# Sliding-window attention beside its projections: both heads' value products in one step, wider splits, keys staged earlier, new step rates

## The chip, the cores and the metric

The kernel runs on one core of one Trainium2 chip. The metric is the device time of one execution in microseconds, median of several runs. The engines are TensorE (PE, with its weight loads shown as PEld), VectorE (DVE), ScalarE (ACT), GpSimd (POOL) and SyncE (SP), which issues the transfers.

## The reference, cut to what matters

The whole program is a two-layer block, a second mixing block and a final norm, all in float32. The change lies in the second layer of the first block ("layer b"), which is attention over a window of 128 tokens, 16 meta tokens and a sink, with a gate:

```python
q, gate = jnp.split(rms_norm(x, norm_g) @ w_in, 2, axis=-1)      # 512+16 tokens, 2048 + 2048 columns
q = partial_rope(q.reshape(B, L, B_Q_HEADS, B_HEAD_DIM), cos, sin)   # 32 query heads of 64, 4 key heads
sr = jnp.einsum('bnqkgd,bnskd->bnkgqs', qr, kb) * scale          # per chunk of 64 queries: 16 + up to 192 keys
sr = jnp.where(valid, sr, -jnp.inf)
pr = sink_softmax(sr, sink)       # exp(sc - m) / (sum exp(sc - m) + exp(sink - m))
orr = jnp.einsum('bnkgqs,bnskd->bnqkgd', pr, vb)
return x + (o * jax.nn.silu(gate)) @ w_out
```

## The kernel before, in words

**Products.** A float32 operand is split into a high part of a narrower format (made on ACT by a copy) and the remainder (made on DVE by a subtraction), and each product is made of three TensorE products: high by high, low by high, high by low. `split` is the helper (L470 on ACT, L471 on DVE; with a scale L473 and L474); the weights get the same at L377 and L378 in `w_split`.

**Units of layer b.** The projection runs in eight units, `q0 g0 q1 q2 g1 q3 g2 g3`: four q units (query columns of four head pairs each) and four g units (their gates). A unit has 4 tiles of 128 columns, a tile has 16 contraction steps of three 512-column products (`pj`); each contraction step ends with `K.tick()`, so a unit has 64 ticks. A tile's sum stands in one of three PSUM banks (`psj`, tag pj). A q tile is rotated on DVE into `f` (two buffers, L972 to L975) and then split into `qp` (L1154), of which there is one set for each of the two tile pairs and heads, shared by consecutive q units; so a q unit's splits wait until the attention of the unit before has made its last scores.

**Attention as a background.** `attention(u, qp)` is a generator. `K.tick` adds `K.rate` to a credit and runs one step of the generator in front for each whole credit. Its steps are, for each of 8 windows n: two transposing steps `trans(n, g)` (one for each of the two key heads g), the scores of window n + 2, and two value steps `values(n, 0)` and `values(n, 1)`. Scores go to one PSUM tile S, transposes to one of two tiles T, values of both heads to the two halves of one bank O (`psO`, one buffer). `values` makes four O products for windows of 208 keys (high and low weights, two key blocks), then copies half the result on ACT (L1116) and adds the other half on DVE into `K.H` (L1117). `K.pe.strict` ties the first projection product that follows a background step in program order behind that step's last TensorE instruction. Apart from such ties and from data, the framework orders the instructions of each engine ahead of the run, by program order and by what is ready in its own estimate; so a later background step may stand ahead of an earlier one that is blocked.

**Windows.** `windows(p)` runs in the background too, once for units 0 and 1 and once for units 2 and 3. It loads the pair's keys (`ke`, from DRAM scratch `kvd`), splits them with a scale (`kxh`, `kxl`), loads the values (`vx`), waits four steps, and transposes and splits the values into `vw`, two windows a step. `ke`, `vx` and the softmax weights `p` share a ring of two buffers (tag "p"). At a q unit's start all but the last background generator are run to their end at once (`while len(K.bg) > 1: K.step()`).

**Gates.** Once attention of unit u is done, each of its four H tiles is multiplied by its gate (L1167), 14 of the 16 on POOL.

Of the kernel before, what the change touches and what calls it, by code (L numbers as in the profile page):

```python
# [10 lines left out]
F32 = mybir.dt.float32  # L11
# [933 lines left out]
def layer_b(K, dbg):  # L945
    nc, tc, a = K.nc, K.tc, K.a
    with ExitStack() as c:
# [46 lines left out]
        for k in range(KT):  # L994
            K.split(K.OPH[:, k], K.OPL[:, k], K.H[:, k], scale=K.vcol("b_norm", k))

        kv = {}
        K.rate = 1 / 5
        done = set()
        pending = {}  # L1000
# [1 line left out]
        def windows(p):  # L1002

            ks = []
            for g in range(2):
                ke = bp.tile([P, TX], F32, tag="p", name="ke", bufs=2)
                for i in range(2):
                    nc.sync.dma_start(ke[64 * i:64 * i + 64], K.kvd[p][64 * g:64 * g + 64])
                kxh = bp.tile([P, TX], R, tag=f"kxh{g}", name="kxh")
                kxl = bp.tile([P, TX], R, tag=f"kxl{g}", name="kxl")  # L1010
                K.split(kxh, kxl, ke, scale=SC_B)
                ks.append((kxh, kxl))
            vx = bp.tile([P, TX], F32, tag="p", name="vx", bufs=2)
            nc.sync.dma_start(vx, K.kvd[2 + p])
            for _ in range(4):
                yield
            vw = bp.tile([P, 2, 8, 2, 2, 64], R, tag="vw", name="vw")
            kv[p] = (ks, vw)

            def vsplit(d, src):  # L1020
                v = src.rearrange("p (g c) -> p g c", g=2)
                K.split(d[:, :, 0], d[:, :, 1], v)
            for n in range(8):
                off, ln = WIN[n]
                t = psT.tile([P, 512], F32, tag="T", name="T")
                n0 = min(ln, P)
                K.pe.transpose(t[0:n0, 0:P], vx[:, off:off + n0], K.ident)
                if ln > P:
                    K.pe.transpose(t[0:ln - P, P:2 * P], vx[:, off + P:off + ln], K.ident)
                vsplit(vw[0:n0, 0, n], t[0:n0, 0:P])  # L1030
                if ln - P == 16:

                    nc.gpsimd.memset(vw[0:32, 1, n].bitcast(F32), 0.0)
                    src = t[0:16, P:2 * P].rearrange("p (g c) -> p g c", g=2)
                    hi, lo = vw[0:16, 1, n, :, 0], vw[0:16, 1, n, :, 1]
                    nc.scalar.activation(vw[32:48, 1, n, :, 0], src, AF.Copy)
                    K.split(hi, lo, src)
                    nc.vector.tensor_tensor(vw[32:48, 1, n, :, 1], src, hi.bitcast(F32), ALU.subtract)
                elif ln > P:
                    vsplit(vw[0:ln - P, 1, n], t[0:ln - P, P:2 * P])  # L1040
                if n % 2:
                    yield

        def attention(u, qp):
# [5 lines left out]
            def scores(n):  # L1050
                off, ln = WIN[n]
                ps = psS.tile([P, 2, 512], F32, tag="S", name="S")
                for g in range(2):
                    for t in range(2):
                        o, q = ps[:, g, t * ln:(t + 1) * ln], qp[t][g][:, P * n:P * n + P]
                        K.pe.matmul(o, q, ks[g][0][:, off:off + ln], start=True, stop=False)
                        K.pe.matmul(o, q, ks[g][1][:, off:off + ln], start=False, stop=True)
                v = ps[:, :, 0:2 * ln].rearrange("p g (t l) -> p g t l", t=2)
                nb = bp.tile([P, 4], F32, tag="nb", name="nb", bufs=2)
                sums = bp.tile([P, 4], F32, tag="sums", name="sums", bufs=2)  # L1060
                es = bp.tile([P, 4], F32, tag="es", name="es", bufs=2)
                pt = bp.tile([P, 4, 208], F32, tag="p", name="p", bufs=2)
                nc.vector.tensor_reduce(nb.rearrange("p (g t) -> p g t", g=2), v, AX.X, ALU.max, negate=True)
                nc.vector.tensor_tensor(nb, nb, ns, ALU.min)  # L1064
                nc.vector.tensor_tensor(es, nb, ns, ALU.subtract)
                for g in range(2):
                    for t in range(2):
                        j = 2 * g + t
                        K.act(pt[:, j, 0:ln], ps[:, g, t * ln:(t + 1) * ln], AF.Exp, bias=nb[:, j:j + 1],
                              accum_out=sums[:, j:j + 1])  # L1070
                K.act(es, es, AF.Exp)
                nc.vector.tensor_tensor(sums, sums, es, ALU.add)
                nc.vector.reciprocal(sums, sums)
                for j in range(4):
                    if j % 2:
                        nc.scalar.activation(pt[:, j, 0:ln], pt[:, j, 0:ln], AF.Copy, scale=sums[:, j:j + 1])
                    else:
                        nc.vector.tensor_scalar(pt[:, j, 0:ln], pt[:, j, 0:ln], sums[:, j:j + 1], None, ALU.mult)
                st[n] = pt

            def trans(n, g):
                off, ln = WIN[n]
                pt = st[n]
                t_ = psT.tile([P, 512], F32, tag="T", name="T")
                n0 = min(ln, P)
                ph = bp.tile([P, 2, 256], R, tag="ph", name="ph", bufs=2)
                pl = bp.tile([P, 2, 256], R, tag="pl", name="pl", bufs=2)
                for t in range(2):
                    K.pe.transpose(t_[0:n0, P * t:P * (t + 1)], pt[:, 2 * g + t, 0:n0], K.ident)
                    if ln > P:  # L1090
                        K.pe.transpose(t_[0:ln - P, 256 + P * t:256 + P * (t + 1)], pt[:, 2 * g + t, P:ln], K.ident)
                K.split(ph[0:n0, 0], pl[0:n0, 0], t_[0:n0, 0:256])
                if ln - P == 16:
                    nc.gpsimd.memset(ph[0:32, 1].bitcast(F32), 0.0)
                    K.split(ph[0:16, 1], ph[32:48, 1], t_[0:16, 256:512])
                elif ln > P:
                    K.split(ph[0:ln - P, 1], pl[0:ln - P, 1], t_[0:ln - P, 256:512])
                st[n, g] = (ph, pl)

            def values(n, g, po):  # L1100
                off, ln = WIN[n]
                ph, pl = st.pop((n, g))
                n0 = min(ln, P)
                o = po[:, 256 * g:256 * g + 256]
                for b in range(2 if ln > P else 1):
                    m = min(ln - P * b, P)
                    if m == 16:
                        K.pe.matmul(o, vw[0:48, b, n, g].rearrange("p h c -> p (h c)"), ph[0:48, b], start=False, stop=True)
                        continue
                    v = vw[0:m, b, n, g].rearrange("p h c -> p (h c)")  # L1110
                    K.pe.matmul(o, v, ph[0:m, b], start=(b == 0), stop=False)
                    K.pe.matmul(o, v, pl[0:m, b], start=False, stop=(b == (ln > P)))

                r = slice(64 * g, 64 * g + 64)
                vo = K.sumsq[:, 256 * (n % 2):256 * (n % 2) + 256].rearrange("p (j q) -> p j q", j=4)
                nc.scalar.activation(vo[r], o[64 - 64 * g:P - 64 * g].rearrange("p (j q) -> p j q", j=4), AF.Copy)  # L1116
                nc.vector.tensor_tensor(K.H[r, 4 * u:4 * u + 4, NM + 64 * n:NM + 64 * n + 64], vo[r],  # L1117
                                        o[r].rearrange("p (j q) -> p j q", j=4), ALU.add)
# [1 line left out]
            po = {}  # L1120
            seq = [[("s", 0)], [("s", 1)]] + [[]] * 3
            for n in range(8):
                seq += [[("t", n, 0)], [("t", n, 1)], [("s", n + 2)] if n < 6 else [], [("v", n, 0)], [("v", n, 1)]]
            for step in seq:
                for f, *x in step:
                    if f == "s":
                        scores(x[0])
                    elif f == "t":
# [6 lines left out]
            done.add(u)  # L1135
            for f in pending.pop(u, []):
                f()

        for un in UNITS_B:
            u = int(un[1])  # L1140
            if un[0] == "q":
                while len(K.bg) > 1:
                    K.step()
                if u % 2 == 0:
                    K.at(K.tickno + 12 + 1, lambda p=u // 2: K.bg.append(windows(p)))

                qp = [[bp.tile([P, 1024], R, tag=f"qp{g}", name="qp", bufs=2) for g in range(2)] for _ in range(2)]
                for j in range(4):
# [4 lines left out]
                        r, r2 = slice(64 * g, 64 * g + 64), slice(64 - 64 * g, P - 64 * g)  # L1153
                        K.split(x[r], x[r2], f[r, NM:T].rearrange("p (n q) -> p n q", n=8), eng=nc.vector)  # L1154
                K.at(K.tickno + 12, lambda u=u, qp=qp: K.bg.append(attention(u, qp)))
                K.rate = .46 if u < 3 else .52
                K.pe.strict = True
            else:
                for j in range(4):
# [3 lines left out]
                    K.act(th, f[:, NM:T], AF.Tanh, scale=0.5)  # L1163
                    nc.vector.scalar_tensor_tensor(th, th, 1.0, f[:, NM:T], ALU.add, ALU.mult)

                    def gate(th=th, dst=K.H[:, 4 * u + j, NM:T], e=nc.vector if u == 3 and j % 2 else nc.gpsimd):
                        e.tensor_tensor(dst, dst, th, ALU.mult)  # L1167
                    if u in done:
                        gate()
                    else:  # L1170
# [824 lines left out]
```

## Time and profile before

| What | Value |
|---|---|
| median of 3 runs | 2838.5 us (2836.59 to 2840.35) |
| the profiled execution: its own time | 2833.57 us |
| its span, first to last instruction | 2831.8 us |
| mean granted TensorE clock | 0.997 of full |
| busy: PE, DVE, ACT, POOL | 99%, 61%, 47%, 12% of the span |
| DMA | 278.64 MB, mean 98 GB/s |

Durations below come from the one profiled execution, which was 4.9 us shorter than the median of the runs. Times are counted from the start of its span. Layer b's eight units lie between about 1144 and 1605 us. A row of the timeline gives start, duration, engine, line, operation, tiles as out<-in, shapes, and in brackets how long the engine had sat idle before it and which instruction released it.

### The profile page before, as it was taken

The page shows a single profiled execution, that of the slowest core. Times are in us where ns is not written, and L with a number is a line of the kernel's source. Part 1 is how long each engine was busy: PE and PEld are TensorE (multiplying, and loading weights), DVE is VectorE, ACT ScalarE, POOL GpSimd, SP SyncE. Part 2 cuts the span into 40 slices and gives each one's busy share as a digit, 9 for nine tenths or more (in the row PEclk, how much of TensorE's full clock was granted, in tenths as well). Part 3 has the DMA queues.
Part 4 walks back from the last instruction along what each step waited for, and adds up shares of the span by engine and source line. Part 5 has one row for each costly group of instructions (what it writes and reads, how often), then busy time and mean ns, then how long its engine had stood idle before and what let it go on. Part 6 is the DMA issues. An engine that isn't in the chain of part 4 may idle for free. (4 is left out here: it accounts for less than half of the span.)

```text
span 2831.8 us, 45345 instructions
## 1 busy us (share of the span) xinstructions
PE 2790.1 (99%) x17576; PEld 2508.1 (89%) x17576; DVE 1713.6 (61%) x3551; ACT 1321.7 (47%) x2973; POOL 329.3 (12%) x362
## 2 busy tenths in 40 slices
PE   9999999999999999999999999999999999999997
PEld 9999999999999999888788888888888887878887
DVE  6555555556575555776767633565656489773375
ACT  5333334334354343564666533465555366552263
POOL 0000000000000110000000022132322134121103
PEclk9999999999999999999999999999999999999999
DMA  5222222222224445312222343322222223233331
GB/s 169 93 75 86 85 75 85 86 76 85 78 78 140 151 133 172 110 67 83 80 75 68 110 144 127 99 83 81 85 77 91 87 92 114 84 106 122 105 112 68
DMA packets 93897, 278.64 MB, mean 98 GB/s; under 512 B 10528, under 2 KB 18864, under 8 KB 93680
## 3 DMA queue, kind: packets, MB, share of 16 engines
q1 hardware_dynamic: 92720, 274.86, 29.9%
q8 instruction: 138, 2.26, 0.3%
q10 hardware_dynamic: 960, 0.87, 0.1%
q14 instruction: 79, 0.65, 0.1%
HBM read 257.11 MB, written 17.01 MB: 97 GB/s over the span
## 5 line engine op out<-in xcount | busy, mean ns | idle before, releaser
L258 PE MATMUL pj<-OPH,wh 128*128 128x264 f32 (+1 forms) x4416 | 1454.5, 331 | 10.1 <-ACT wh L377 6.6
L258 PE MATMUL pj<-OPH,wl 128*128 128x264 f32 (+1 forms) x4416 | 1449.1, 329 | 1.5 <-DVE wl L378 1.5
L258 PE MATMUL pj<-OPL,wh 128*128 128x264 f32 (+1 forms) x4416 | 1446.6, 328 | 0.0
L377 ACT ACTIVATE wh<-wraw 128x512 fp32r<-128x512 f32 (+2 forms) x868 | 544.3, 628 | 969.8 <-PE pj L258 879.4
L378 DVE TENSOR_TENSOR wl<-wraw,wh 128x512 fp32r<-128x512 f32 (+2 forms) x868 | 620.6, 716 | 611.2 <-ACT wh L377 605.1
L258 PEld LDWEIGHTS pj<-OPH,wh 128*128 128x128 f32 x4416 | 830.3, 189 | 85.3 <-ACT wh L377 7.0
L258 PEld LDWEIGHTS pj<-OPL,wh 128*128 128x128 f32 x4416 | 832.5, 189 | 75.1 <-DVE OPL L471 0.2
L258 PEld LDWEIGHTS pj<-OPH,wl 128*128 128x128 f32 x4416 | 832.7, 189 | 70.8 <-DVE wl L378 1.8
L531 POOL TENSOR_TENSOR sumsq<-sumsq,sq 128x512 f32<-128x512 f32 (+2 forms) x86 | 98.8, 1156 | 552.1 <-ACT sq L530 501.6
L258 PE MATMUL pj<-wh,OPH 128*128 128x260 f32 (+1 forms) x384 | 123.5, 322 | 0.0
L258 PE MATMUL pj<-wh,OPL 128*128 128x260 f32 (+1 forms) x384 | 122.8, 320 | 0.0
L258 PE MATMUL pj<-wl,OPH 128*128 128x260 f32 (+1 forms) x384 | 120.7, 320 | 0.0
L851 POOL TENSOR_TENSOR H<-H,th 128x528 f32<-128x528 f32 x3 | 3.9, 1313 | 832.9 <-DVE th L850 791.3
L258 PEld LDWEIGHTS pj<-wh,OPH 128*128 128x128 f32 x384 | 72.2, 188 | 6.6 <-issue 1.5
L258 PEld LDWEIGHTS pj<-wl,OPH 128*128 128x128 f32 x384 | 71.9, 188 | 6.0
L306 ACT ACTIVATE st<-st 128x512 f32<-128x512 f32 (+3 forms) x136 | 72.4, 549 | 9.7 <-DVE st L1213 8.3
L258 PEld LDWEIGHTS pj<-wh,OPL 128*128 128x128 f32 x384 | 72.3, 188 | 5.1
L306 ACT ACTIVATE p<-S,nmx 128x264 f32<-128x264 f32 (+5 forms) x112 | 49.8, 449 | 45.6 <-DVE nmx L737 33.2
L470 ACT ACTIVATE ph<-T 80x256 fp32r<-80x256 f32 (+3 forms) x128 | 49.7, 392 | 27.7 <-DVE pl L471 12.7
L261 PE MATMUL T<-ident,p 128*128 128x128 f32 (+3 forms) x392 | 60.1, 271 | 1.0 <-DVE p L1853 0.9
L306 ACT ACTIVATE p<-S,nb 128x208 f32<-128x208 f32 (+2 forms) x128 | 51.2, 412 | 20.7 <-DVE nb L1064 20.5
L471 DVE TENSOR_TENSOR pl<-T,ph 128x256 fp32r<-128x256 f32 (+2 forms) x120 | 51.5, 433 | 8.9 <-ACT ph L470 7.8
(449 smaller groups left out, 3344.0 us busy)
## 6 DMA issues: line engine op xcount, KB each, us to landing
wraw<-in_w SPq DMA_DIRECT2D x410, 512.0 KB, 3.5
xr<-in_x SPq DMA_DIRECT2D x32, 264.0 KB, 3.8
wraw<-in_w SPq DMA_DIRECT2D x16, 520.0 KB, 3.5
xr<-hd SPq DMA_DIRECT2D x32, 256.0 KB, 2.8
hd<-H SPq DMA_DIRECT2D x16, 264.0 KB, 2.0
hd<-H SPq DMA_DIRECT2D x16, 256.0 KB, 2.0
wraw<-in_w SPq DMA_DIRECT2D x16, 256.0 KB, 2.8
wraw<-in_w SPq DMA_DIRECT2D x7, 384.0 KB, 5.0
```

Source lines behind the costliest of these rows:

```text
L258: return self._put(self.nc.tensor.matmul(*args, **kw))
L261: return self._put(self.nc.tensor.transpose(*args, **kw))
L306: i = self.nc.scalar.activation(out, in_, func, **kw)
L377: nc.scalar.activation(h[:, 0:kc * n], raw, AF.Copy)
L378: nc.vector.tensor_tensor(l[:, 0:kc * n], raw, h[:, 0:kc * n].bitcast(F32), ALU.subtract)
L470: nc.scalar.activation(hi, src, AF.Copy)
L471: eng.tensor_tensor(lo, src, hi.bitcast(F32), ALU.subtract)
L531: (eng or nc.gpsimd).tensor_tensor(acc[:, c0:c1], acc[:, c0:c1], sq[:, c0:c1], ALU.add)
L851: nc.gpsimd.tensor_tensor(dst, dst, th, ALU.mult)
```

## The change

1. **Values in one step.** The step list now has, for each window, two transposing steps, the scores of window n + 2, an empty step, and one step with `values(n, 0)` and `values(n, 1)`. The number of steps stays 45.
2. **Two key blocks split at once.** In windows of 208 keys the second key block is transposed as 128 columns instead of 80 (the excess is the next head's weights, or a strip `pw[:, 832:880]` that POOL clears; it is not used later), so that one split of 128x512 takes the place of one of 128x256 and one of 80x256.
3. **Keys staged.** The second pair's `windows` generator is advanced twice from within unit 1's attention, in the steps where windows 6 and 7 have no scores to start; each time it loads and splits one head's keys. It now yields after each of the two.
4. **Densities.** `K.rate` was .46 until q3's end and .52 after; it is .48 in g0 and g1, .40 in q1, q2 and q3, and .58 in g2 and g3.
5. **Gates.** All gates run on VectorE; those that wait for a unit's attention take one step each instead of all together.

`vw` changes from `[P, 2, 8, 2, 2, 64]` to `[P, 15, 2, 2, 64]`, with index `7 * b + n` for block b; those lines are left out here.

```diff
-        kv = {}
+        kv, staged = {}, {}
...
                 ks.append((kxh, kxl))
+                if p and not g:
+                    yield
+            if p:
+                yield
             vx = bp.tile([P, TX], F32, tag="p", name="vx", bufs=2)
...
-                pt = bp.tile([P, 4, 208], F32, tag="p", name="p", bufs=2)
+                pw = bp.tile([P, 880], F32, tag="p", name="p", bufs=2)
+                pt = pw[:, 0:832].rearrange("p (j l) -> p j l", j=4)
+                if ln > 144:
+                    nc.gpsimd.memset(pw[:, 832:880], 0.0)
...
                     K.pe.transpose(t_[0:n0, P * t:P * (t + 1)], pt[:, 2 * g + t, 0:n0], K.ident)
-                    if ln > P:
+                    if ln == 208:
+
+                        o = 208 * (2 * g + t) + P
+                        K.pe.transpose(t_[:, 256 + P * t:256 + P * (t + 1)], pw[:, o:o + P], K.ident)
+                    elif ln > P:
                         K.pe.transpose(t_[0:ln - P, 256 + P * t:256 + P * (t + 1)], pt[:, 2 * g + t, P:ln], K.ident)
-                K.split(ph[0:n0, 0], pl[0:n0, 0], t_[0:n0, 0:256])
+                if ln == 208:
+                    K.split(ph, pl, t_.rearrange("p (b q) -> p b q", b=2))
+                else:
+                    K.split(ph[0:n0, 0], pl[0:n0, 0], t_[0:n0, 0:256])
                 if ln - P == 16:
                     nc.gpsimd.memset(ph[0:32, 1].bitcast(F32), 0.0)
                     K.split(ph[0:16, 1], ph[32:48, 1], t_[0:16, 256:512])
-                elif ln > P:
-                    K.split(ph[0:ln - P, 1], pl[0:ln - P, 1], t_[0:ln - P, 256:512])
...
-                seq += [[("t", n, 0)], [("t", n, 1)], [("s", n + 2)] if n < 6 else [], [("v", n, 0)], [("v", n, 1)]]
+                seq += [[("t", n, 0)], [("t", n, 1)], [("s", n + 2)] if n < 6 else [("w",)],
+                        [], [("v", n, 0), ("v", n, 1)]]
             for step in seq:
                 for f, *x in step:
+                    if f == "w":
+                        if u == 1:
+                            next(staged[1])
+                        continue
...
             for f in pending.pop(u, []):
                 f()
+                yield
 
         for un in UNITS_B:
             u = int(un[1])
+            if un != "q0":
+                K.rate = .58 if u > 1 and un[0] == "g" else .40 if un[0] == "q" else .48
             if un[0] == "q":
                 while len(K.bg) > 1:
                     K.step()
                 if u % 2 == 0:
-                    K.at(K.tickno + 12 + 1, lambda p=u // 2: K.bg.append(windows(p)))
+                    staged[u // 2] = windows(u // 2)
+                    K.at(K.tickno + 12 + 1, lambda p=u // 2: K.bg.append(staged[p]))
...
-                K.rate = .46 if u < 3 else .52
...
-                    def gate(th=th, dst=K.H[:, 4 * u + j, NM:T], e=nc.vector if u == 3 and j % 2 else nc.gpsimd):
-                        e.tensor_tensor(dst, dst, th, ALU.mult)
+                    def gate(th=th, dst=K.H[:, 4 * u + j, NM:T]):
+                        nc.vector.tensor_tensor(dst, dst, th, ALU.mult)
```

## Rows read from the trace of the kernel before

**Rows 1.** The page: length of the span; busy time of TensorE, share, instructions.

```profile
span 2831.8 us, 45345 instructions
PE 2790.1 (99%) x17576; PEld 2508.1 (89%) x17576; DVE 1713.6 (61%) x3551; ACT 1321.7 (47%) x2973; POOL 329.3 (12%) x362
```

**Rows 2.** Busy time by stretch: a late one without attention, g1's, layer b's sum.

```profile
1600.00:1650.00 50.00, 50.00 (x217) 40.42 (x216) 23.25 (x36) 20.46 (x33) 7.12 (x6) 1.00 0.51 170
...
1361.00:1420.00 59.00, 54.81 (x279) 45.36 (x279) 44.01 (x95) 34.00 (x92) 4.58 (x4) 1.00 0.27 87
...
sum 444.00, PE 434.48 PEld 360.51 DVE 316.55 ACT 262.05 POOL 23.61; mean PE 54.31 PEld 45.06 DVE 39.57 ACT 32.76 POOL 2.95
```

**Rows 3.** Waits of TensorE from 1190 to 1600 us: total, times, longest.

```profile
PE O L258 <- DVE H L1117: 6.1, 7, 1.7
PE S L258 <- ACT kxh L473: 2.0, 1, 2.0
PE pj L258 <- DVE sh L973: 1.4, 1, 1.4
```

**Rows 4.** Timeline around the waits of g1 and of q3 into g2.

```profile
1370.82 0.27 PE L258 MATMUL S<-kxl,qp 128*128 128x208 f32 x1
...
1376.29 0.39 PE L258 MATMUL O<-ph,vw 128*128 128x256 f32 x1 [0.80 <-DVE H L1117]
...
1377.05 0.69 DVE L972 TENSOR_TENSOR f<-pj,trigb 128x512 f32<-128x512 f32 x1
...
1378.44 0.50 PE L258 MATMUL pj<-OPH,wh 128*128 128x512 f32 x1 [1.40 <-DVE sh L973]
...
1393.72 0.67 ACT L473 ACTIVATE kxh<-ke 128x560 fp32r<-128x560 f32 x1 [1.25 <-DMA ke<-kvd]
...
1394.44 0.31 PE L258 MATMUL S<-kxh,qp 128*128 128x80 f32 x1 [1.99 <-ACT kxh L473]
...
1488.51 0.38 PE L258 MATMUL O<-ph,vw 128*128 128x256 f32 x1 [1.65 <-DVE H L1117]
```

**Rows 5.** Timeline, from unit 2's last O product to its result in H.

```profile
1513.88 0.28 PE L258 MATMUL O<-pl,vw 80*128 80x256 f32 x1
...
1514.20 0.38 ACT L1116 ACTIVATE sumsq<-O 64x256 f32<-64x256 f32 x1 [1.22 <-PE O L258]
...
1514.61 0.42 DVE L1117 TENSOR_TENSOR H<-sumsq,O 64x256 f32<-64x256 f32 x1 [0.91 <-ACT sumsq L1116]
```

**Rows 6.** Timeline, unit 3, window 7, from the first head's values to the second's.

```profile
1588.99 0.28 PE L258 MATMUL O<-pl,vw 80*128 80x256 f32 x1
...
1590.12 0.41 DVE L1117 TENSOR_TENSOR H<-sumsq,O 64x256 f32<-64x256 f32 x1
...
1590.58 0.38 PE L258 MATMUL O<-ph,vw 128*128 128x256 f32 x1 [0.60 <-DVE H L1117]
```

**Rows 7.** Timeline, unit 1, window 2, between the first head's values and the second's.

```profile
1348.40 1.04 PE L261 MATMUL T<-ident,p 128*128 128x128 f32 x8
...
1349.19 0.34 PE L258 MATMUL S<-kxh,qp 128*128 128x208 f32 x1
...
1350.16 0.29 PE L258 MATMUL O<-ph,vw 128*128 128x256 f32 x1
```

**Rows 8.** Timeline of VectorE: two consecutive tiles of q1 read from PSUM.

```profile
1294.91 0.69 DVE L972 TENSOR_TENSOR f<-pj,trigb 128x512 f32<-128x512 f32 x1 [0.72 <-PE pj L258]
...
1302.79 0.68 DVE L972 TENSOR_TENSOR f<-pj,trigb 128x512 f32<-128x512 f32 x1
```

**Rows 9.** Groups by line, layer b: busy us, mean ns, idle before.

```profile
L471 DVE TENSOR_TENSOR pl<-T,ph 128x256 fp32r<-128x256 f32 (+1 forms) x112 | 46.0, 415 | 8.0 <-ACT ph L470 6.8
...
L470 ACT ACTIVATE ph<-T 128x256 fp32r<-128x256 f32 (+2 forms) x120 | 44.9, 379 | 26.4 <-DVE pl L471 12.7 <-PE O L258 10.3 <-PE T L261 2.0
...
L1167 POOL TENSOR_TENSOR H<-H,th 128x512 f32<-128x512 f32 x14 | 20.9, 1511 | 235.8 <-DVE H L1117 191.5 <-DVE th L1164 44.3
...
L1167 DVE TENSOR_TENSOR H<-H,th 128x512 f32<-128x512 f32 x2 | 1.4, 693 | 0.1
```

## What is predicted

> **What bounds the kernel now.** Read the page first: TensorE is busy 2790.1 of 2831.8 us [rows 1], so at most 41.7 us in the whole program are there to be won by removing waits. The change touches layer b alone, so the second view is the busy time by stretch, cut at the units from q0's end to g3's: TensorE is busy 434.48 of 444 us, DVE 316.55 (71%), ACT 262.05 (59%), at full granted clock, and g1's stretch alone loses 4.2 of the 9.5 us that TensorE is idle [rows 2]. The third view, TensorE's waits in the layer, accounts for all of it with nine waits [rows 3]: seven of O products for DVE's L1117 (6.1 us), one of scores for the split keys (2.0 us), one of a projection product for DVE's L973 (1.4 us). The rest is TensorE's own work: without attention beside it a product of 512 columns starts every 50.00/217 = 0.230 us [rows 2]. So three things can move the time: these waits, new waits, and TensorE work. The timelines of the waits, read last, say what each hangs on.
>
> **TensorE's work stays.** The change takes away no TensorE instruction. The second block's transposes now have 128 columns of weights instead of 80, but the moving operand stays the 128-column identity, and eight transposes, alternately 128 and 80 wide, take (1349.19 - 1348.40)/8 = 0.10 us each [rows 7]; 0, and if wider weights cost in proportion to their 48 columns, 0.10 x 48/128 x 96 = +3.6 us. I take 0.
>
> **Keys staged.** Attention of unit 2 waited 1.99 us for the second pair's keys, whose split on ACT ended at 1394.39 after a wait for their DMA [rows 4]. In the new order the keys are asked for some 20 to 30 ticks before unit 2's first scores, at least 20 x 3 x 0.230 = 14 us, so transfer and split are over: -2.0 us (bounds -2.0 and 0). The two loads of each head go past weight transfers on SP's queue in either version; TensorE waits for no weights [rows 3]. Next late would be the values' load, now after the keys' yields; only value products need it, nine steps later.
>
> **From one window's values to the next.** O has one bank, so the next window's first O product waits for the last L1117. Two waits were of this kind, 0.80 and 1.65 us [rows 4]. Now an empty step lies between, which at a rate near .45 is 2.2 ticks or 2.2 x 3 x 0.230 = 1.5 us of products: the first wait goes, the second shrinks to 0.1. -2.4 us (bounds -2.4 and 0).
>
> **From one head's values to the other's.** This speaks against the change. The other five O waits, 6.1 - 0.80 - 1.65 = 3.7 us, lie between the heads of one window. In unit 3's window 7 the second head's first product starts 0.05 us after the first head's L1117 ended (1590.12 + 0.41), having waited 0.60 us [rows 6], although it writes the other half of the bank. So the second head's values follow the first's only after the copy on ACT and the add on DVE. Undisturbed, this chain takes from the start of the last O product to L1117's end 1514.61 + 0.42 - 1513.88 = 1.15 us [rows 5], with one DVE operation of 0.69 us in its way half the time 1.5 us. Before, two ticks, 6 x 0.230 = 1.4 us of projection products, lay between by the step list. Now none does, since the product behind a background step stays behind it. What can still cover the chain is what the framework pulls forward while the second head is blocked: in unit 1's window 2, eight transposes and eight score products stood there, 1350.16 - 1348.40 = 1.76 us [rows 7]; and products of the next tile: q1's third and fourth tile were read 1302.79 - 1294.91 = 7.9 us apart, where 48 products take 11.0 us [rows 8], so some 13 products of the fourth ran before the third ended.
>
> Count it. Windows 0 to 4 of each unit have transposes and scores to pull: cover 1.76 + 0.12 (the last O product) against 1.55, no wait. Windows 5 and 6 have no scores left to start, cover 0.79 + 0.12: 0.64 us x 8 = 5.1. Window 7 has nothing, 1.55 - 0.12 = 1.43 us x 4 = 5.7. Of these 10.8 us I let products of the next tile cover half: 5.4. Against the 3.7 us of before that is +1.7 us. Bounds: all covered -3.7; nothing ever covered, 32 x (1.15 + 0.05 - 0.12) = 34.6, or +31.
>
> A rule bears on this. That the second head waits is in [rows 6]; were it only that row's accident, and the two halves independent, the term would be -3.7. The Trainium skill, page "PSUM — Partial Sum Buffer", section "PSUM bank collisions raise a hardware error", says that accesses are to be kept apart by bank and quadrant, since another address in the same bank still collides. By that rule no half is ever independent, and the term lies between my +1.7 and the +31.
>
> **PSUM banks in g1.** Unit 2's queries go into `qp` only after unit 1's last scores; till then q2's third and fourth tile keep two PSUM banks, g1's first tile takes the third, and g1's second tile waits: 1.40 us at 1378.44, 7.6 us after the last scores at 1370.82, with q2's evacuation at 1377.05 [rows 4]. Those scores are the 33rd step. Counted from tick 12 of q2, at .46 throughout they fell at tick 12 + 32/.46 - 64 = 17.6 of g1; at .40 for 52 ticks and then .48 they fall at 12 + 52 + (32 - 20.8)/.48 - 64 = 23.3. That is 5.7 ticks, 5.7 x 3 x 0.230 = 3.9 us later, if the framework pulled nothing forward; but it pulls attention forward whenever products are blocked, as the cluster in [rows 7] shows, which also stands in q2. And DVE and ACT have fewer attention steps in q2. +1 us (bounds -1.4 and +3.9). The same shift in q3 has slack: g2 had no such wait [rows 3].
>
> **Work run at q3's start.** By the credits, unit 1's attention makes its last values at tick 48 of g1 and its three waiting gates by tick 54, and q3 begins with the four steps of `windows(1)` that transpose values and unit 2's first scores still in the queue; they now come at once. They are 15 transposes with about 15 split pairs, each near 0.28 + 0.28 us on ACT and DVE by the 379 and 415 ns of 256-column ones [rows 9], taken down for half the columns; ACT and DVE work side by side, so about 15 x 0.3 = 4.5 us if TensorE stood still. Only the last of these instructions, a score product, ties the products behind it, and T has two buffers, so most of it lies beside projection products. +0.5 us (bounds 0 and +4.5).
>
> **Splits, gates, clears: off the path.** One split of 128x512 for two: 48 times DVE 0.69 (the 512-column read of PSUM at L972 [rows 4]) for 2 x 0.415, -6.7 us; on ACT 48 x (2 x 0.379 - about 0.63, scaled like DVE's) = -6 us. Gates: 14 x 0.693 = +9.7 us on DVE, -20.9 us on POOL [rows 9]. DVE gains 3 us of 316.55, ACT loses 6 of 262.05; both had over a quarter of the stretch free [rows 2], and TensorE's work covers them. Without that cover a gate delays what queues behind it on DVE (L1117, weight remainders) by 0.69 us each time: +9.7 at worst, but the gates now come one a step. POOL's 24 clears lie beside the scores' maxima. A transpose that reads 48 columns of the next head's weights waits for one more scaling, over steps earlier. Taken at 0 (bounds -2 and +5).
>
> **Sum.** -2.0 - 2.4 + 1.7 + 1 + 0.5 = -1.2 us. The profiled execution took 2833.57 us, so 2832.4 by its own clockwork; the runs' median lay 4.9 us higher, and against that, 2838.5, it is 2837 us. About 0.2% (5.7 us) is what a measurement of this kernel tells from no change.
>
> **The rivals.**
> *All waits go.* Key, bank and window waits vanish and the heads' chain is covered everywhere: -9.5 us, 2829 us. For it: the nine waits are all that TensorE loses, and the new densities spread attention where DVE also rotates queries. Against: two ticks of cover are taken away 32 times. It needs the heads' new waits below 9.5 - 5.7 = 3.8 us in all. Chance 0.31.
> *The heads' chain lies open.* Place: the second head's first O product in each window. It decides from (5.7 + 2.0 + 2.4 + 3.7 - 1.5)/32 = 0.38 us a window; at 0.8 us it is 25.6 - 3.7 - 2.9 = +19, 2857 us, at 0.55 us +11, 2849.5 us; at full price +28. For it: [rows 6], and 1.55 us against little cover in windows 5 to 7. Against: windows 0 to 4 have the cluster of [rows 7]. Chance 0.22.
> *The PSUM banks hold g1 up.* The full 3.9 us there and 4.5 us at q3's start: -1.2 + 2.9 + 4 = +5.7, 2844 us. Chance 0.07.
> *Nothing that can be told.* The forecast, -5.7 to +5.7 us, 2833 to 2844: the gains and the new wait are of one size. Chance 0.40.
>
> **The numbers.** The likeliest case gives 2837. Faster by over 0.2% is the first rival, 0.31; same 0.40; slower, the second and third, 0.29. The range takes in the first rival and its -2 of free cover, 2827, and the second up to 0.55 us a window, 2850; what lies beyond that, and below, is about 0.15.
>
> **What would show it.** In the waits of TensorE: the row of scores for L473 gone; the row of O for L1117 with more, shorter waits, nearly all at a second head's first product, and most in windows 5 to 7; the row of products for L973 near or above 1.4 us. In the lines: L1167 on DVE 16 times, L471 48 times at 128x512. The prediction is wrong if O's waits exceed some 12 us or fall under 2, if a wait of another kind above 4 us appears in layer b, or if the time moves outside this layer.

## The result, and the profile after

The changed kernel takes 2857.06 us (median of 4 runs, 2856.71 to 2858.56) against 2838.32 us for the kernel before in the same session: a ratio of 1.007 [1.0057, 1.0082], 18.7 us slower. The forecast was 2837 us, its range 2827 to 2850. The time is the one that the second rival gave, the chain between the heads lying open.

The head of the page after, and below it TensorE's waits in layer b (columns: waiter, releaser, us in all, times, longest). [rows 1] and [rows 3] answer to them.

```profile
span 2854.9 us, 45322 instructions
PE 2801.0 (98%) x17576; PEld 2518.4 (88%) x17576; DVE 1707.0 (60%) x3517; ACT 1316.7 (46%) x2925; POOL 311.7 (11%) x372
```

```profile
PE T L261 <- DVE pl L471: 12.5, 6, 3.9
PE O L258 <- DVE H L1129: 6.6, 4, 2.6
PE S L258 <- ACT p L306: 1.8, 1, 1.8
PE pj L258 <- DVE wl L378: 1.0, 2, 0.8
PE T L261 <- DVE vw L471: 0.5, 1, 0.5
```

The profiled execution of after took 2856.71 us, 23.1 more than that of before. From the first product of layer b's projection to the start of the evacuation that ends g3, before needs 461.7 us and after 484.3, 22.6 more; the rest of the program takes 2370.1 and 2370.7 us. So the loss lies in layer b, and it has two parts. TensorE's idle stretches above 0.1 us, nearly all of them in the view above, sum to 22.5 us, against 9.5 [rows 3]: +13.0. The other part is TensorE's busy time over the same work (columns here and below: stretch, length, then busy us and instructions of PE, PEld, DVE, ACT and POOL, granted clock as a share of 2.4 GHz, DMA share, GB/s). Before, then after:

```profile
1144.00:1605.00 461.00, 451.48 (x2309) 374.29 (x2308) 329.90 (x742) 270.41 (x767) 23.61 (x23) 1.00 0.24 78
```

```profile
1144.00:1628.40 484.40, 461.87 (x2303) 382.66 (x2302) 324.87 (x706) 265.49 (x718) 6.13 (x33) 0.97 0.23 75
```

TensorE is busy 10.4 us longer with as many instructions. The clock column says why: 0.97. In after the granted clock falls to 0.50 (1.2 GHz) six times in this layer, for 27.3 us together, and before not once. TensorE is busy for 23.3 of these 27.3 us. In one of the falls a product of 512 columns starts every 0.43 us (from 1389.86 us), and as soon as it is over every 0.23 us (from 1391.87 us). The first of these falls, with the stretch before it and the one behind:

```profile
1276.00:1282.50 6.50, 3.94 (x22) 3.08 (x20) 4.13 (x9) 2.19 (x4) 0.00 (x0) 1.00 0.37 103
1282.50:1285.90 3.40, 3.35 (x10) 2.87 (x11) 2.64 (x4) 2.23 (x4) 0.00 (x0) 0.50 0.29 117
1285.90:1290.00 4.10, 4.10 (x20) 3.30 (x19) 1.38 (x4) 1.26 (x2) 0.00 (x0) 1.00 0.00 0
```

TensorE was idle for 2.56 of the 6.50 us ahead of it. In the 3.40 us at half clock it starts 10 instructions, in the next 4.10 us 20.

That wait is the chain between two heads, in unit 0's window 6. The timeline of after (start, duration, engine, line, operation, tiles, shapes, in brackets the idle time and the releaser) runs from the first head's last O product to the second head's first:

```profile
1279.43 0.28 PE L258 MATMUL O<-pl,vw 80*128 80x256 f32 x1
...
1279.56 0.38 PE L261 MATMUL T<-ident,p 128*128 128x128 f32 x2
...
1279.69 0.60 ACT L470 ACTIVATE ph<-T 128x512 fp32r<-128x512 f32 x1
...
1280.30 0.67 DVE L378 TENSOR_TENSOR wl<-wraw,wh 128x512 fp32r<-128x512 f32 x1
1280.32 0.38 ACT L1128 ACTIVATE sumsq<-O 64x256 f32<-64x256 f32 x1
...
1280.89 0.68 DVE L471 TENSOR_TENSOR pl<-T,ph 128x512 fp32r<-128x512 f32 x1
1281.49 0.68 DVE L974 TENSOR_TENSOR sh<-sh,trigb 128x512 f32<-128x512 f32 x1
1282.09 0.40 DVE L1129 TENSOR_TENSOR H<-sumsq,O 64x256 f32<-64x256 f32 x1
...
1282.55 0.58 PE L258 MATMUL O<-ph,vw 128*128 128x256 f32 x1 [2.61 <-DVE H L1129]
```

Two things are to be seen. The copy (L1128) starts behind another ACT operation, and the add (L1129) stands behind three DVE operations of 0.67 to 0.68 us; from the last O product to the add's end it is 1282.09 + 0.40 - 1279.43 = 3.06 us, not 1.55. And the cover is two transposes. In unit 2's window 4 DVE has the splits of query tiles in front:

```profile
1497.99 0.28 PE L258 MATMUL O<-pl,vw 80*128 80x256 f32 x1
1498.11 0.27 PE L261 MATMUL T<-ident,p 128*128 128x128 f32 x1
...
1498.62 2.00 DVE L471 TENSOR_TENSOR qp<-f,qp 64x512 fp32r<-64x512 f32 x3
...
1500.85 0.69 DVE L471 TENSOR_TENSOR qp<-f,qp 64x512 fp32r<-64x512 f32 x1
1501.57 0.69 DVE L471 TENSOR_TENSOR pl<-T,ph 128x512 fp32r<-128x512 f32 x1
...
1502.18 0.40 DVE L1129 TENSOR_TENSOR H<-sumsq,O 64x256 f32<-64x256 f32 x1
1502.32 1.11 PE L261 MATMUL T<-ident,p 128*128 128x128 f32 x4 [3.93 <-DVE pl L471]
1503.08 0.56 PE L258 MATMUL O<-ph,vw 128*128 128x256 f32 x1
```

Four transposes were pulled ahead of the second head here, but there are two T tiles, and a T tile is free only when its split has been made, which stands behind the query splits too. So the waiter that the profile names is a transpose, not an O product, though it stands in the same place and is itself in the O product's way. So the row of waits for L1129 shows only part of this chain. Sorted by place instead (TensorE's idle stretches above 0.1 us, put between the O products around them), after has 16.4 us between the two heads of a window, of which 6.7 us end at an O product, 8.7 us at a transpose and 1.0 us at a projection product. Of the 15.4 us at O products and transposes 12.7 lie in windows 0 to 4, and 2.7 in windows 5 to 7. Before, O products had waited 3.7 us between the heads, and all products, with the one wait for keys and the one for a PSUM bank, 7.1 us. In 12 of the 32 windows of after no projection product at all lies between the heads; before this was so in none. The other 6.1 us of after are a wait of 3.79 us between windows 4 and 5 of unit 1, at the end of q2, and 2.3 us at q3's start. Around the first of these no projection product starts from 1379.92 to 1389.27 us, since g1's first tile is complete and its second has no PSUM bank yet; the transposes there wait for a split that stands behind four query splits on ACT and on DVE.

### The profile page after: what moved, and what is told of

Same layout as the page of the kernel before. It is cut to its first block, busy times and chain, and to the rows that moved or that the text cites. A ratio compares the mean times of both kernels' runs of the same rounds, so it can differ in the third digit from the quotient of the medians.

```text
span 2854.9 us, 45322 instructions
## 1 busy us (share of the span) xinstructions
PE 2801.0 (98%) x17576; PEld 2518.4 (88%) x17576; DVE 1707.0 (60%) x3517; ACT 1316.7 (46%) x2925; POOL 311.7 (11%) x372
## 5 line engine op out<-in xcount | busy, mean ns | idle before, releaser
L261 PEld LDWEIGHTS T<-ident,p 128*128 128x128 f32 (+3 forms) x392 | 44.4, 133 | 21.6 <-DVE pl L471 11.9
L471 DVE TENSOR_TENSOR pl<-T,ph 128x512 fp32r<-128x512 f32 (+2 forms) x72 | 45.0, 627 | 17.8 <-ACT ph L470 16.6
```

Of the source, the lines that this page charges most:

```text
L261: return self._put(self.nc.tensor.transpose(*args, **kw))
L471: eng.tensor_tensor(lo, src, hi.bitcast(F32), ALU.subtract)
```

## The experiments

Times are medians, ratios are against runs of the kernel before on the same chip, with their 95% intervals. The waits are TensorE's in layer b, of one profiled execution each.

### The two heads in one step

Undone alone in the changed kernel (`e1_after_heads_apart`):

```diff
-                        [], [("v", n, 0), ("v", n, 1)]]
+                        [("v", n, 0)], [("v", n, 1)]]
```

> The changed kernel with each head's values in a step of its own again, two ticks apart; all other edits kept. Theory H (the second head's values wait for the first head's copy and add on the same PSUM bank, and the joined step left nothing between them; the clock falls after the longer waits): between-heads waits fall from about 15 to under 5 us, the granted clock goes back above 0.995, 2836 to 2842 us. Rival W (the wide split holds a transpose tile too long, as the 12.5 us of transposes waiting for L471 suggest): those waits stay near 12 us, 2853 to 2858 us. Rival D (the new densities crowd attention into stretches where VectorE is full): 2850 to 2858 us.

Made alone in the kernel before (`e3_before_heads_joined`):

```diff
-   [("s", n + 2)] if n < 6 else [], [("v", n, 0)], [("v", n, 1)]]
+   [("s", n + 2)] if n < 6 else [], [], [("v", n, 0), ("v", n, 1)]]
```

> The kernel before with only the joined step (empty step, then both heads' values). Theory H: TensorE's waits in layer b rise from 9.5 to 18 to 25 us, dips of the granted clock appear in the layer, 2848 to 2860 us. Rivals W and D: this edit is harmless, 2834 to 2843 us.

The step joined, but the products of both heads put ahead of both copies and adds, in the changed kernel, where the joined step is kept (`e2_after_products_first`), and in the kernel before, where it is made as above (`e7_before_products_first`):

```diff
+            def settle(n, g, po):
+                o = po[:, 256 * g:256 * g + 256]
...                       (the copy and the add, unchanged, now belong to settle)
                         values(x[0], x[1], po[x[0]])
+                        if x[1]:
+                            settle(x[0], 0, po[x[0]])
+                            settle(x[0], 1, po[x[0]])
```

> The changed kernel with the joined step kept, but both heads' eight products issued ahead of both heads' copy and add. Theory H: no second head waits any more, O's waits for the add fall under 2 us, clock above 0.995, 2828 to 2838 us. Rivals W and D: the step itself is not the cause, waits of transposes for L471 stay near 12 us, 2850 to 2858 us.

> The kernel before with the joined step and both heads' products issued ahead of both heads' copy and add; nothing else of the change. Theory H: no head waits for the other, O's waits under 3 us, 2830 to 2836 us. Rival: the wait only moves to the next window's first product, which now has two evacuations ahead of it: O's waits 5 us or more, 2837 to 2842 us.

| Run | us | ratio | waits, us | us at 1.2 GHz | layer b, us |
|---|---|---|---|---|---|
| after | 2857.06 | 1.007 [1.0057, 1.0082] | 22.5 | 27.3 | 484.3 |
| heads apart | 2838.39 | 1.0005 [0.9996, 1.0015] | 11.1 | 3.4 | 461.4 |
| after, products first | 2839.62 | 1.0006 [0.9997, 1.0015] | 8.3 | 6.8 | 463.3 |
| before, heads joined | 2850.31 | 1.0051 [1.0036, 1.0066] | 18.7 | 13.7 | 479.8 |
| before, products first | 2833.36 | 0.9987 [0.9977, 0.9996] | 5.0 | 6.8 | 458.7 |

One line of the step list gives the whole loss back, and nearly all falls of the clock go with it; between the heads TensorE then waits 4.9 us instead of 16.4. Made alone it costs 12 us (the execution that was profiled took 2855.34 us, 5 more than the median). Of the 9.2 us of new waits there 5.9 stand in one row, which in the kernel before was 6.1 us in 7 [rows 3]:

```profile
PE O L258 <- DVE H L1117: 12.0, 14, 1.4
```

And with the same step, as empty of projection products, but the products first, nothing is lost: so not the missing products are the cost, but the copy and the add between the two heads' products. The changed kernel with products first lies 1.6 us above what was expected; 2.6 us of its waits are at one O product at q2's end, and the same wait stands in the best kernel once it has the new rates (below).

### The wide splits

Alone in the kernel before (`e4_before_wide_split`), and taken out of the changed kernel (`e6_after_narrow_split`):

```diff
...                       (the transposes of 128 columns, the strip and the index of vw, as in the change)
+                if ln == 208:
+                    K.split(ph, pl, t_.rearrange("p (b q) -> p b q", b=2))
+                else:
+                    K.split(ph[0:n0, 0], pl[0:n0, 0], t_[0:n0, 0:256])
```

> The kernel before with only the wide splits (second block transposed as 128 columns, one split of 128x512, smaller value tile). Theory H: nothing that can be told, 2834 to 2843 us, transposes wait for L471 under 2 us. Rival W: transposes wait for L471 by 8 us or more, 2846 to 2857 us. Rival D: as H.

> The changed kernel with the two narrow splits of before, all else kept. Rival W: the pulled-forward transposes no longer wait for L471, 2846 to 2852 us, transposes' waits under 4 us. Theory H with the rates: the wide split is harmless or a gain of 4 us, so 2856 to 2862 us, with the waits moved from the transposes back to O's.

Alone: 2833.23 us, 0.9987 [0.9978, 0.9997], 5 us faster. Taken out of the changed kernel: 2850.65 us, 1.0045 [1.0032, 1.0059], so inside the joined step the wide splits cost about 6 us. They were taken at 0 in the prediction, and the sign depends on what stands beside them. TensorE's waits without them, in the changed kernel:

```profile
PE O L258 <- DVE H L1121: 13.0, 9, 3.9
PE T L261 <- DVE pl L471: 4.1, 1, 4.1
```

Between the heads they are 13.6 us instead of 16.4, and nearly all at O products: with narrow splits the transposes get through while the add is late, and the second head's own product waits instead. The clock is at half for 13.7 us instead of 27.3, and in the layer TensorE is busy 5.0 us less and waits 2.7 us less.

Both good parts together, in the kernel before (`e8_wide_products_first`):

> The kernel before with the wide splits and with the joined step whose products come first; rates, keys and gates of before. Theory H: both gains hold, 2826 to 2833 us, waits in layer b under 6 us. Rival: the wide split was all there was to gain, 2832 to 2837 us.

2831.48 us, 0.9978 [0.9969, 0.9986]: faster than both kernels. No O product waits any more; the waits left are

```profile
PE S L258 <- ACT kxh L473: 4.3, 1, 4.3
PE pj L258 <- DVE es L1068: 0.8, 1, 0.8
PE S L258 <- ACT p L306: 0.6, 2, 0.4
```

and eight O products run without a gap, 0.12 us apart, where the second head's four begin at 1236.93 (timeline):

```profile
1236.81 0.28 PE L258 MATMUL O<-pl,vw 80*128 80x256 f32 x1
1236.93 0.28 PE L258 MATMUL O<-ph,vw 128*128 128x256 f32 x1
```

### Step rates, and the tie

The old rates in the changed kernel (`e5_after_old_rates`), and the new rates on the best kernel (`e11_best_new_rates`):

```diff
-            if un != "q0":
-                K.rate = .58 if u > 1 and un[0] == "g" else .40 if un[0] == "q" else .48
...
+                K.rate = .46 if u < 3 else .52
```

> The changed kernel with the rates of before (.46, then .52), joined step kept. The joined step alone cost 12 us on the kernel before, the whole change 19. Theory H with the rates adding the rest (unit 1's last scores fall later, so that the products of g1 run out of PSUM banks): 2848 to 2853 us, the waits near 1380 us in g1 under 3 us. Rival W (the joined step is dearer here because the wide split holds the transposes that are pulled between the heads): the rates change nothing, 2854 to 2859 us.

> The same base, with the new densities. Theory: the lower rate in q2 puts unit 1's last scores 5.7 ticks later and g1 waits for PSUM banks by 1 to 4 us more, 2832 to 2837 us. Rival: nothing, 2829 to 2832 us, as putting the old rates back in the changed kernel did nothing.

With the old rates the changed kernel takes 2856.33 us, 1.0068 [1.0052, 1.0083]: no difference. Its waits only change places: the 3.79 us at q2's end shrink to 0.38, and between the heads it waits 23.1 us instead of 16.4. In all it waits 25.3 us instead of 22.5, but at half clock it is for 13.7 us instead of 27.3. On the best kernel, where there is no such exchange, the new rates cost some 7 us: 2838.99 us, 1.0004 [0.9995, 1.0013], with 9.1 us of waits for 5.6. That is above both expectations, and the new wait is not where it was expected: at q2's end it is 4.9 us for the best kernel's 5.1, and new are 3.9 us at unit 3's second scores (1518.52 us), which wait for the softmax of its first window.

The changed kernel without the tie of the next projection product to a background step (`e12_after_untied`):

```diff
-                K.pe.strict = True
```

> The changed kernel without the tie that keeps a projection product behind the background product ahead of it. Theory H: the tie is what leaves TensorE with nothing to do while a second head waits; untied, the framework fills those places with projection products and the waits between heads fall under 6 us, 2836 to 2846 us. Rival: the background products, always last in line, now come late and the waits move to the units' ends, 2850 us or more.

2849.85 us, 1.004 [1.0025, 1.0055], above what was expected. Between the heads it waits 9.7 us instead of 16.4, where under 6 was expected; 2.5 of these stand behind the layer. Layer b ends after 458.6 us, as short as in the best kernel, but attention is not done by then, and the rest of the program takes 2391 us instead of 2370. The view of waits from 1150 to 1640 us:

```profile
PE T L261 <- DVE pl L471: 9.5, 5, 4.6
PE O L258 <- DVE H L1129: 4.6, 4, 1.8
PE pj L258 <- ACT OPH L473: 2.3, 1, 2.3
```

Of these the waits for L1129 (but 0.3 us) and L473 stand at 1631 to 1640 us. The tie thus makes part of the wait between the heads, but without it attention is late at the end: 26 us less in the layer, 21 us more behind it.

### Keys and gates, on the best kernel

Keys staged as in the change (`e9_best_keys_staged`), and all gates on DVE, one a step (`e10_best_gates_vector`):

```diff
-  [("s", n + 2)] if n < 6 else [], [], [("v", n, 0), ("v", n, 1)]]
+  [("s", n + 2)] if n < 6 else [("w",)], [], [("v", n, 0), ("v", n, 1)]]
...
+                    if f == "w":
+                        if u == 1:
+                            next(staged[1])
+                        continue
...                       (the two yields and `staged`, as in the change)
```

> The kernel before with wide splits and products first (0.9978 of before), and the second pair's keys staged from within unit 1. If the staging does what it says, the 4.3 us wait of unit 2's scores for the split keys goes and the dip of the clock with it: 2825 to 2829 us. Rival: the wait goes elsewhere (PSUM banks in g1, the scores' own buffer), 2830 to 2834 us.

```diff
-    e.tensor_tensor(dst, dst, th, ALU.mult)
+    nc.vector.tensor_tensor(dst, dst, th, ALU.mult)
...
             for f in pending.pop(u, []):
                 f()
+                yield
```

> The same base, with all gates on VectorE and one gate a step. Theory: off the path, 2829 to 2834 us. Rival: the gates hold VectorE's adds and weight remainders up, 2835 to 2840 us, with new waits behind L1167 or L378.

Keys staged: 2830.41 us, 0.9974 [0.9964, 0.9984], not to be told from the best kernel. The wait for the keys, which it was to remove, stayed. The timeline shows where it comes from:

```profile
1374.84 0.60 PE L261 MATMUL T<-ident,p 128*128 128x128 f32 x4
...
1375.47 7.81 SPq L1008 DMA_DIRECT2D ke<-kvd  x4
...
1379.24 0.67 ACT L473 ACTIVATE kxh<-ke 128x560 fp32r<-128x560 f32 x1
...
1379.96 0.43 PE L258 MATMUL S<-kxh,qp 128*128 128x80 f32 x1 [4.52 <-ACT kxh L473]
```

The load is issued 0.03 us after the transposes of `p` end (1374.84 + 0.60), and `ke` and `p` share a ring of two buffers. In the kernel before the two are as close (1382.63 and 1382.66), in the changed one too (1388.55 and 1388.59). So the load is as early as the buffer is free, wherever it is put in the step list. That reading wasn't tried with a buffer of its own.

Gates on DVE: 2834.66 us, 0.9985 [0.9977, 0.9994]; its interval overlaps that of the best kernel, so a cost of some 3 us is not excluded.

## Why the prediction was wrong

**The step that failed is "From one head's values to the other's", +1.7 us.** The waits there rose from 3.7 us to 15.4 (6.7 + 8.7), +11.7, and the two experiments that move this step alone show that the term carries the loss. The rule of the chain held: the second head's products do wait for the first head's copy and add. Mis-sized were the chain's length and its cover.
- The chain was priced at 1.15 us or, with one DVE operation in its way, 1.55. From the start of the first head's last O product to the end of its add it measured 2.14 us on the mean of the 32 windows, and 4.59 at the longest. The change did not make it so: in the kernel before the mean was 1.94 us already, the longest 4.38, and [rows 5] shows one of the shortest. What stands in its way is DVE's queue: query splits (2.00 + 0.69 us), rotation, weight remainders.
- Windows 0 to 4 were counted as covered, by the eight transposes and eight scores of [rows 7], and so priced at 0. That was one favourable window. A transpose needs one of two T tiles, and a T tile is freed by a split that stands in the same DVE queue; the cover was late for the same reason as the chain. Of the 15.4 us, 12.7 came here, in windows 0, 2, 3 and 4.
- Windows 5 to 7, where the prediction put all of its 5.4 us, waited 2.7. Products of the next tile were missing elsewhere: of the 12 windows with none between the heads, nine are among windows 0 to 4. So the place was wrong too, and not only the size.

The longest chain in the kernel before, unit 2's window 0 (timeline), where the copy stands behind the softmax on ACT and the add behind a rotation and a weight remainder on DVE; the second head waits although transposes and scores were pulled between:

```profile
1433.86 0.28 PE L258 MATMUL O<-pl,vw 80*128 80x256 f32 x1
...
1436.55 0.38 ACT L1116 ACTIVATE sumsq<-O 64x256 f32<-64x256 f32 x1
...
1437.86 0.38 DVE L1117 TENSOR_TENSOR H<-sumsq,O 64x256 f32<-64x256 f32 x1
...
1438.29 0.39 PE L258 MATMUL O<-ph,vw 80*128 80x256 f32 x1 [0.99 <-DVE H L1117]
```

**What no term stood for** is the granted clock: 10.4 us of busy time in after, nearly half the loss. The rival's 0.8 us a window is met only with it: the waits alone are 15.4/32 = 0.48 us a window, for which the rival's own sum gives 15.4 - 3.7 - 2.9 = +8.8 us, 2847 us. Its mechanism was right; that its time was met is in part luck. No run here has the waits without the clock's falls, so the two are told apart only as rows of one trace, and how the loss divides is not fixed: with the old rates there is more waiting and half as much time at half clock, at the same time in all.

**The rule on PSUM**, from the Trainium skill, page "PSUM — Partial Sum Buffer", section "PSUM bank collisions raise a hardware error", put the term above +1.7 (both halves lie on the same 128 partitions, so a rule by bank and quadrant covers them), and the trace agrees: in all 32 windows the second head's first O product starts 0.05 us or more after the end of the first head's add, which reads the other half of the bank. The rows show that the product waits for DVE, not what would happen if it did not: no run lets the second head start beside the first head's copy and add, or gives each head a bank of its own. The eight products 0.12 us apart show that TensorE's own writes to the two halves don't hold each other up.

**The other terms:**
- TensorE's work, 0: right at full clock. With the heads apart, and all else as in after, it is busy 449.89 us in 461.00.
- Keys staged, -2.0: the wait is gone, the reason was wrong. Staged on the best kernel it stays at 4.5 us; with the new rates and nothing staged it falls to 0.3. In after unit 2's first scores come at 1407.57 us, long after the load.
- The next window's values, -2.4, and the PSUM banks in g1, +1: the waits of 1.65, 0.80 and 1.40 us [rows 4] are gone, but 3.79 us stand at q2's end. This is the delay by the lower rate that was worked out at 3.9 us and then taken down to 1: unit 1's last scores come after 816 of the layer's projection products, in the kernel before after 801. With the old rates it is 801 and 0.38 us. The rate is not all that decides it, since the best kernel, at the old rates, has 816 too.
- Work run at q3's start, +0.5: 2.3 us, within its bounds.
- Splits, gates, clears, 0: durations and counts as worked out (below), but the splits are worth -5 us alone and +6 in the joined step, and the new rates, not priced by themselves, cost 7 us on the best kernel.

The groups of lines of after for the splits and gates (mean ns is the figure after the busy us):

```profile
L471 DVE TENSOR_TENSOR pl<-T,ph 128x512 fp32r<-128x512 f32 x48 | 32.9, 687 | 12.4 <-ACT ph L470 11.2
L1187 DVE TENSOR_TENSOR H<-H,th 128x512 f32<-128x512 f32 x16 | 10.5, 683 | 0.1
```

**The pieces add up:** after with products first is the best kernel with keys staged, gates on DVE and the new rates. It lies 8 us above the best one, and the rates alone lie 7 above it.

**What stays open:** whether a third buffer for the keys would take away the 4.3 us of the best kernel; whether the second head would wait if its values stood in another PSUM bank; and which waits bring the clock down.

## What to carry to other kernels

When two steps that write to one PSUM bank are joined, put all their products ahead of all their evacuations; the same joining costs 12 us in the one order and saves 5 in the other. Cover that a scheduler is to pull forward has to be checked for what it needs itself: if its buffers are freed by the queue that makes the wait, it is no cover. Price a chain by all its rows and not by one: 1.15 us was among the shortest of 32 in the kernel before, whose mean was 1.94. On a kernel that is 98% TensorE, new waits can cost more than their length, if the granted clock falls with them: here 13.0 us more of waits came with 10.4 us more of busy time, 1.7 times the waits in all. In the other three kernels where the copy and the add stand between joined heads and the tie is kept, layer b grew by 1.4 to 2.0 times the new waits.

## What was not expected of the hardware

The granted clock of a TensorE that is busy 95% of a stretch falls to 1.2 GHz around single short waits. In after the falls come with waits of 1.81 to 3.93 us, while waits of 1.99 and 1.65 us [rows 4] had none before, and in the changed kernel with the heads apart one of 2.54 us had none; with the heads joined in the kernel before a wait of 0.96 us at 1516.4 had one. So the length of a single wait doesn't decide it. What it costs is read from the rows: 27.3 us at half clock, in 4.0 of which TensorE is idle, against 10.4 us more of busy time.
